# RWKV chunk chain in one product for both heads, and its group norm along the free axis

## The chip, the cores and the metric

The kernel runs on one core of a Trainium2 chip. The metric is the time of one execution on the device in microseconds (us), the median of three runs. The names of the engines are those of the profile: PE is TensorE (PEld its weight loads), DVE is VectorE, ACT is ScalarE, POOL is GpSimd and SP is SyncE, which issues most DMAs.

## The reference

One decoder block with 512 tokens and 2048 channels in fp32: RMS norm, an input projection `w_in`, RWKV-7 time mixing (16 heads of 64) beside sliding-window attention, a gated merge through `w_out`, then a gated ConvFFN. The change touches the RWKV part alone:

```python
def step(state, inp):
    r_t, k_t, v_t, w_t, ka_t, kb_t = inp
    sa = jnp.einsum('bhvk,bhk->bhv', state, ka_t)
    state = (state * w_t[:, :, None, :] + sa[..., None] * kb_t[:, :, None, :]
             + v_t[..., None] * k_t[:, :, None, :])
    y = jnp.einsum('bhvk,bhk->bhv', state, r_t)
    return state, y
...
mu = jnp.mean(y, axis=-1, keepdims=True)
var = jnp.mean(jnp.square(y - mu), axis=-1, keepdims=True)
y = ((y - mu) * lax.rsqrt(var + GN_EPS)).reshape(B, S, RW_DIM)
y = y * gn_w.astype(f32) + gn_b.astype(f32)
bonus = jnp.sum(rh * kh * r_k.astype(f32), axis=-1, keepdims=True) * vh
out = (y + bonus.reshape(B, S, RW_DIM)) * g.astype(f32)
```

The state is 64 x 64 per head; the mean and variance are over a head's 64 channels.

## The kernel before

The 512 columns of a tile are tokens and its 128 partitions channels, that is two heads of 64, a pair; there are `NP` = 8 pairs. The tokens are cut into `NCH` = 8 chunks of `C` = 64. In the stretch of the change TensorE does two kinds of work:

- **The projections.** Each of 70 z tiles (`ztile`, `project`) is 48 products of 128x128 weights with 512 columns into a PSUM tile `acc` (L260, L261, L262: weights and input each in a high and a low part, three products). A weight tile comes by a DMA on SP (`raw`, L240), ACT makes its high part `whi` (L243) and DVE the low part `wlo` (L244); three such pairs of tiles are held, each good for 12 products. After every third weight load `sums_along` issues one copy in DRAM on SP (L227) and one accumulating DMA on POOL that waits for it (L228).
- **The RWKV work of a pair**, in three functions. `early(p)` projects k, r and v, makes the decays and gates, normalises `kk` (its column statistics by `head_stats`, L378, and `head_rows`, L381 and a trip through DRAM). `late(p)` is the chunk algorithm. `final(p)` is the group norm and the output `o_rw_d`.

The loop is `late(p)`, `early(p+1)`, `final(p)`, three gate tiles (`emit_gate`), for each pair. The order on each engine is not the program's: a scheduler fixes it when the kernel is built, from priorities and readiness, so products of the projections are placed between those of the chain; only what `pin` marks keeps its place. Queues run in the order so fixed.

`late(p)` before: it forms `BKK` (keys) and `BAR` (queries, per head `h` and kind `a`, with zeros in the other head's partitions), and for each chunk the product of both (L689, four to a PSUM tile). DVE masks it into `AB` (strictly causal, L692) and `MM` (causal, L693). In each head's half of the partitions the own head's block is copied to `BX` (L698) and its place in `AB` is refilled with `BAR` (L700); so `AB` and `SV` together hold for each head its chunk-crossing and its state part one above the other. `BX` is then inverted by five levels of fp16 products and transposes (L728 to L730, L751). `KK` and the values in `UV` and `SV` come by transposes (L715, L719). The chain is eight serial steps:

- psG (L758): per head a product with 64 output columns of the array, into that head's half of the partitions; DVE copies it to `G` (L760).
- psU (L762): one product with `BX` (block-diagonal); ACT copies one head's half to `UV` (L763), DVE the other (L764).
- psS (L769): per head again; DVE adds it to the decayed state `SV` (L771), one operation per head.

The outputs (L779, L781) are per head too, two products each, channel-major, into one PSUM tile `bulk`; `split` cuts them into `yhl`. `final` centres them by two products with a constant (L789, L790), squares, takes statistics with L378, `rsqrt_small` on DVE, and spreads the factors back over channels with `head_rows`: a transpose (L381), a store and two loads in DRAM on SP; then four DVE operations (L799 to L804). The PSUM ring `bulk` has three tiles, the chain's ring two.

Of the kernel before, what the change touches and what calls it, by code (L numbers as in the profile page):

```python
# [18 lines left out]
P = 128  # L19
# [3 lines left out]
C = 64  # L23
# [11 lines left out]
class Dims:  # L35
# [38 lines left out]
    ("ident", 128), ("strict", 64), ("incl", 64), ("istack", 64),  # L74
    ("m1", 64), ("m2", 64), ("m4", 64), ("m8", 64), ("m16", 64), ("m32", 64),
    ("t1bd", 128), ("idsg", 128), ("tri", 128), ("bo", 128), ("cen", 128), ("sel2", 2), ("ones", 128), ("dist", 256),
# [9 lines left out]
def shape_constants():  # L86
    out = np.zeros((P, NCONST), np.float32)

    def put(nm, a):
        o, n = CONST_AT[nm]  # L90
        out[:, o : o + n] = a

    i = np.arange(P)
    put("ident", np.eye(P))
    s = (i % C)[:, None]
    t = np.arange(C)[None, :]
    put("strict", s < t)
    put("incl", s <= t)
# [10 lines left out]
    put("cen", (si == ti) - same / float(C))  # L109
# [25 lines left out]
def block_kernel(ctx: ExitStack, tc: tile.TileContext, d: Dims, a: dict, out: bass.AP):  # L135
# [136 lines left out]
    bor = cstp.tile([P, P], F32R, name="bor")  # L272
    cenr = cstp.tile([P, P], F32R, name="cenr")
# [9 lines left out]
    if True:  # L283
# [69 lines left out]
        pin(act.activation(bor, K["bo"], AF.Copy))  # L353
        pin(act.activation(cenr, K["cen"], AF.Copy))
# [162 lines left out]
        with ExitStack() as pr:  # L517
# [56 lines left out]
            pool.memset(BAR[0:C, :, 1], 0.0)  # L574
            pool.memset(BAR[C:P, :, 0], 0.0)
            AB, MM, KK, SV, UV = (bd.tile([P, NCH, 2, C], F32, name=n) for n in ("AB", "MM", "KK", "SV", "UV"))
            pool.memset(SV[0:C, 0, 0], 0.0)
            pool.memset(SV[C:P, 0, 1], 0.0)
# [20 lines left out]
            def early(p):  # L599
# [56 lines left out]
                dve.tensor_tensor(bon, vz, ps, op=ALU.mult)  # L656
                return ag, Ei, kk, kb, k2, rz, vz, bon

            def late(p, st):
# [3 lines left out]
                for h, (lo, hi) in enumerate(HV):  # L663
                    ol, oh = HV[1 - h]
                    hs = slice(lo, hi)
                    dve.tensor_tensor(BKK[hs, :, lo:hi], kb3[hs], Ei3[hs], op=ALU.mult)
                    dve.tensor_tensor(BKK[hs, :, ol:oh], k23[hs], Ei3[hs], op=ALU.mult)
                    dve.scalar_tensor_tensor(BAR[hs, :, h, 0], kk3[hs], -1.0, Eex[hs], op0=ALU.mult, op1=ALU.mult)
                    dve.tensor_tensor(BAR[hs, :, h, 1], rz3[hs], Ein[hs], op=ALU.mult)
                    act.activation(BV[hs, :, ol:oh], vz3[hs], AF.Copy)  # L670
# [14 lines left out]
                dve.tensor_tensor(BKE, BKK, ee.unsqueeze(2).to_broadcast([P, NCH, P]), op=ALU.mult)  # L685
                for n0 in range(0, NCH, 2):
                    ps = bulk().rearrange("p (q c) -> p q c", c=P)
                    for j in range(2):
                        pe.matmul(ps[:, 2 * j : 2 * j + 2].rearrange("p q c -> p (q c)"), BKK[:, n0 + j],  # L689
                                  BAR[:, n0 + j].rearrange("p h a c -> p (h a c)"), start=True, stop=True)  # L690
                    q2 = lambda t: t[:, n0 : n0 + 2].rearrange("p n h c -> p (n h) c")
                    dve.tensor_tensor(q2(AB), ps[:, :, 0:C], mb("strict", 4), op=ALU.mult)  # L692
                    dve.tensor_tensor(q2(MM), ps[:, :, C:P], mb("incl", 4), op=ALU.mult)  # L693
                for g in range(2):
                    ns = slice(g * HN, (g + 1) * HN)
                    for h, (lo, hi) in enumerate(HV):
                        own = AB[lo:hi, ns, h]
                        (dve.tensor_copy if h else act.copy)(BX[lo:hi, ns, lo:hi], own)  # L698
                        dve.tensor_tensor(tt[lo:hi, ns], own, mb("m1", HN, (lo, hi)), op=ALU.mult)
                        act.copy(own, BAR[lo:hi, ns, h, 0])  # L700
                    dve.tensor_tensor(tt[:, ns], tt[:, ns], mb("istack", HN), op=ALU.add)
                    split(X[:, 0, ns], X[:, 1, ns], tt[:, ns])
                    ps = bulk().rearrange("p (n c) -> p n c", c=P)
                    for j in range(HN):
                        pe.transpose(ps[:, j], BX[:, g * HN + j], ident)
                    at_ = wk.tile([P, HN, P], F32, name="at_", tag="at_")
                    dve.scalar_tensor_tensor(at_, ps, SG, mb("idsg", HN), op0=ALU.mult, op1=ALU.add)
                    split(AI[:, 0, ns], AI[:, 1, ns], at_)
                    for i in range(2):
                        dve.tensor_tensor(BT[:, i, ns], AI[:, i, ns], mb("t1bd", HN), op=ALU.mult)  # L710
                for g in range(2):
# [43 lines left out]
                for n in range(NCH):  # L755
                    ps = chn.tile([P, C], F32, name="psG", tag="chn")
                    for h, (lo, hi) in enumerate(HV):
                        pe.matmul(ps[lo:hi], AB[:, n, h], SV[:, n, h], start=True, stop=True)  # L758
# [3 lines left out]
                    pe.matmul(ps, BX[:, n], G, start=True, stop=True)  # L762
                    act.activation(UV[0:C, n, 0], ps[0:C], AF.Copy)  # L763
                    dve.tensor_copy(UV[C:P, n, 1], ps[C:P])  # L764
                    if n == NCH - 1:
                        break
                    ps = chn.tile([P, C], F32, name="psS", tag="chn")
                    for h, (lo, hi) in enumerate(HV):
                        pe.matmul(ps[lo:hi], KK[:, n, h], UV[:, n, h], start=True, stop=True)  # L769
                    for h, (lo, hi) in enumerate(HV):  # L770
                        dve.scalar_tensor_tensor(SV[lo:hi, n + 1, h], SV[lo:hi, n, h], ee[lo:hi, n : n + 1], ps[lo:hi],  # L771
                                                 op0=ALU.mult, op1=ALU.add)


                ps = bulk()
                for n in range(NCH):
                    for h, (lo, hi) in enumerate(HV):
                        dst = r3(ps)[lo:hi, n]
                        pe.matmul(dst, UV[:, n, h], MM[:, n, h], start=True, stop=n == 0)  # L779
                        if n:  # L780
                            pe.matmul(dst, SV[:, n, h], BAR[:, n, h, 1], start=False, stop=True)  # L781
                yhl = wk.tile([P, 2, S], F32R, name="yhl", tag="rhl")
                split(yhl[:, 0], yhl[:, 1], ps)
                return ag, bon, yhl

            def final(p, st):
                ag, bon, yhl = st
                ps = bulk()
                pe.matmul(ps, cenr, yhl[:, 0], start=True, stop=False)  # L789
                pe.matmul(ps, cenr, yhl[:, 1], start=False, stop=True)  # L790
                yc = wtile("yc")
                dve.tensor_copy(yc, ps)
                sq = wtile("gn")
                act.activation(sq, ps, AF.Square)
                ps = bulk()
                head_stats(ps, sq)
                rs = rsqrt_small(wk, ps[:, 0 : 2 * NT], 1.0 / HD, GN_EPS)
                rb = head_rows(wk, bulk(), rs, "gn")
                dve.tensor_tensor(yc, yc, rb, op=ALU.mult)  # L799
                dve.tensor_scalar(yc, yc, col("gn_w", p), col("gn_b", p), op0=ALU.mult, op1=ALU.add)  # L800
                dve.tensor_tensor(yc, yc, bon, op=ALU.add)
# [605 lines left out]
```

## Time and profile before

| | |
|---|---|
| median of three runs | 2952.3 us (2951.39 to 2952.68) |
| profiled execution, its span | 2946.4 us |
| TensorE busy | 2897.7 us (98%) |
| VectorE busy | 1949.0 us (66%) |
| ScalarE busy | 1316.0 us (45%) |
| mean granted TensorE clock | 0.997 |
| first psG to last | 352.3 to 1193.5 us |

The profiled execution's time is its span; the median is from other runs. A row of the groups gives line, engine, operation, what it writes and reads, the tile sizes and a count, then busy time and mean ns of one, then idle time before them and what ended it. In the timeline, a row is a start and a length in us; `x4` are four records merged. An fp32 product appears as two records, a product in the projections' format or in fp16, and a transpose, as one. `128*64` is rows and columns of the array that are in use. Records overlap: a start is nearer to the cost than a length.

### The profile page before, as it was taken

To read this page: it belongs to the slowest core of one execution; us is meant where nothing else is said; L and a number is where in the kernel's file an instruction comes from. 1 tells how busy PE (TensorE), PEld (TensorE's weight loads), DVE (VectorE), ACT (ScalarE), POOL (GpSimd) and SP (SyncE) were. 2 spreads that over 40 slices of the span, in tenths; PEclk is the share of its full clock that TensorE was granted. 3 is DMA by queue.
4 is the path that set the end of the run, shared out by engine and by line. 5 is a ranking of instruction groups with operands and counts; after the bars stand their busy time and mean duration, and the time that the engine had idled before them with its cause. 6 is when DMAs were issued, how large, how long until landed. Compare 5 with 4: busy or idle time off the path is not lost.

```text
span 2946.4 us, 48467 instructions
## 1 busy us (share of the span) xinstructions
PE 2897.7 (98%) x18922; PEld 2473.2 (84%) x18922; DVE 1949.0 (66%) x3242; ACT 1316.0 (45%) x2134; POOL 219.4 (7%) x286
## 2 busy tenths in 40 slices
PE   7999999999999999999999899999999999999999
PEld 6777777777777777688888899999999999888887
DVE  5555666666666666344567877778777778665555
ACT  4344434434334334232346554554554555544444
POOL 0001000000000000101000011011011011000000
PEclk9999999999999999999999999999999999999999
DMA  6855656656656656878877788888888888877775
GB/s 185 210 151 153 178 139 154 159 129 161 158 131 162 155 129 170 250 223 262 275 243 247 193 242 236 230 227 225 234 239 235 227 229 237 311 240 242 256 258 189
DMA packets 225142, 609.47 MB, mean 207 GB/s; under 512 B 24768, under 2 KB 44944, under 8 KB 223888
## 3 DMA queue, kind: packets, MB, share of 16 engines
q1 hardware_dynamic: 157504, 434.92, 45.9%
q0 software_dynamic: 36064, 132.14, 23.3%
q10 hardware_dynamic: 31344, 39.31, 3.9%
q8 instruction: 148, 2.42, 0.3%
q14 instruction: 82, 0.67, 0.1%
HBM read 556.62 MB, written 174.43 MB: 248 GB/s over the span
## 4 chain that ended last, share of the span: by engine, by line
PE 92%; DVE 3%; ACT 2%; DMA 2%; issue 1%; ACTq 0%; SPq 0%; DVEq 0%
PE X L1108 17%; PE X L975 11%; PE acc L262 10%; PE acc L261 10%; PE acc L260 10%; PE Y L975 8%; PE Y L1108 8%; PE Z L1108 4%; PE psG L758 1%; PE bulk L689 1%; PE mi L505 1%; PE bulk L751 1%; PE psS L769 1%; PE bulk L728 1%; DMA raw<-in_w_z_dram 1%
## 5 line engine op out<-in xcount | busy, mean ns | idle before, releaser
L262 PE MATMUL acc<-xhi,wlo 128*128 128x512 f32 x1120 | 460.0, 411 | 0.7 <-DVE wlo L244 0.7
L260 PE MATMUL acc<-xhi,whi 128*128 128x512 f32 x1120 | 454.9, 406 | 4.0 <-ACT whi L243 4.0
L261 PE MATMUL acc<-xlo,whi 128*128 128x512 f32 x1120 | 453.9, 405 | 0.0
L243 ACT ACTIVATE whi<-raw 128x512 fp32r<-128x512 f32 x352 | 220.0, 629 | 491.3 <-PE acc L261 326.2
L968 DVE TENSOR_TENSOR wlo<-raw,whi 128x1024 fp32r<-128x1024 f32 x210 | 257.0, 1224 | 203.4 <-ACT whi L967 202.4
L244 DVE TENSOR_TENSOR wlo<-raw,whi 128x512 fp32r<-128x512 f32 x352 | 240.3, 688 | 205.1 <-ACT whi L243 198.1
L967 ACT ACTIVATE whi<-raw 128x1024 fp32r<-128x1024 f32 x210 | 222.6, 1060 | 289.3 <-PE X L975 151.8
L1108 PE MATMUL X<-b,whi 128*128 128x256 f32 x1472 | 270.4, 284 | 2.3 <-DVE u L1128 0.9
L1108 PE MATMUL X<-t,whi 128*128 128x256 f32 x1408 | 258.9, 284 | 8.7 <-DVE u L1128 8.3
L1091 DVE TENSOR_TENSOR wlo<-raw,whi 128x1024 fp32r<-128x1024 f32 x176 | 215.1, 1223 | 77.5 <-ACT whi L1090 77.2
L1108 PE MATMUL Y<-t,whi 128*128 128x256 f32 x1408 | 257.1, 283 | 0.0
L262 PEld LDWEIGHTS acc<-xhi,wlo 128*128 128x128 f32 x1120 | 211.3, 189 | 44.2 <-issue 3.1
L260 PEld LDWEIGHTS acc<-xhi,whi 128*128 128x128 f32 x1120 | 211.6, 189 | 43.2 <-ACT whi L243 5.2
L261 PEld LDWEIGHTS acc<-xlo,whi 128*128 128x128 f32 x1120 | 211.3, 189 | 40.3 <-issue 3.1
L1090 ACT ACTIVATE whi<-a 128x1024 fp32r<-128x1024 f32 x132 | 139.3, 1056 | 216.4 <-DVE a L1084 213.2
L1108 PEld LDWEIGHTS X<-b,whi 128*128 128x128 f32 x1472 | 230.7, 193 | 3.1 <-issue 2.4
L1108 PEld LDWEIGHTS X<-t,whi 128*128 128x128 f32 x1408 | 220.8, 193 | 9.3 <-DVE u L1128 5.7
L1108 PEld LDWEIGHTS Y<-t,whi 128*128 128x128 f32 x1408 | 219.6, 192 | 0.0
L1108 PE MATMUL X<-b,wlo 128*128 128x256 f32 x736 | 209.1, 284 | 2.1 <-DVE wlo L1091 2.1
L1091 DVE TENSOR_TENSOR wlo<-a,whi 128x1024 fp32r<-128x1024 f32 x132 | 161.7, 1226 | 68.2 <-ACT whi L1090 67.6
L1108 PE MATMUL X<-t,wlo 128*128 128x256 f32 x704 | 200.1, 284 | 0.1
L1108 PE MATMUL Y<-t,wlo 128*128 128x256 f32 x704 | 199.2, 283 | 0.0
(346 smaller groups left out, 6151.2 us busy)
## 6 DMA issues: line engine op xcount, KB each, us to landing
raw<-in_w_up_dram SPq DMA_DIRECT2D x180, 512.0 KB
raw<-in_w_z_dram SPq DMA_DIRECT2D x288, 256.0 KB
s_dn<-in_w_dn_dram POOLq DMA_DIRECT2D x88, 512.0 KB, 6.3
raw<-in_w_up_dram POOLq DMA_DIRECT2D x88, 512.0 KB, 8.7
raw<-s_dn SPq DMA_DIRECT2D x88, 512.0 KB
raw<-in_w_dn_dram SPq DMA_DIRECT2D x66, 512.0 KB
a<-in_w_up_dram SPq DMA_DIRECT2D x48, 512.0 KB
s_dn<-in_w_dn_dram SPq DMA_DIRECT2D x44, 512.0 KB
```

The source lines that it names most:

```text
L243: pin(act.activation(hi, raw, AF.Copy))
L244: pin(dve.tensor_tensor(lo, raw, hi.bitcast(F32), op=ALU.subtract))
L260: pe.matmul(acc, whi[:, j], xhi[:, k], start=first, stop=False)
L261: pe.matmul(acc, whi[:, j], xlo[:, k], start=False, stop=False)
L262: pe.matmul(acc, wlo[:, j], xhi[:, k], start=False, stop=last)
L505: pe.matmul(ps[:, h], pT[:, kb, h], vt[:, n - 1 + kb, g * HD : (g + 1) * HD], start=kb == kbs[0], stop=kb == kbs[-1])
L967: act.activation(whi, wr, AF.Copy)
L968: dve.tensor_tensor(wlo, wr, whi.bitcast(F32), op=ALU.subtract)
L975: pe.matmul(dst, l[:, q, ts], r[:, es], start=fst and j == 0, stop=lst and j == 2, skip_group_check=True)
L1090: pin(act.activation(hi, t, AF.Copy))
L1091: pin(dve.tensor_tensor(lo, t, hi.bitcast(F32), op=ALU.subtract))
L1108: pin(pe.matmul(ps, l[:, k], r[:, k], start=start and k + i == 0, stop=last and i == 2, skip_group_check=True))
```

## The change

`AB`, `MM`, `KK`, `SV`, `UV` go. In their place everything of a chunk stands for both heads at once, on 128 partitions, with operands that are block-diagonal or hold a mask's zeros:

- Four masks in place of two split L689's product into `BX` and `OA` (own head's block and the crossing one, strictly causal) and `MD` and `MO` (the same, causal). `BAR` is laid out by kind first, so both heads' queries are one 128-column operand.
- The values are centred over the head's channels at once, and turned to token-major, by a product with a constant (`VV`). What the values add to G (`GV`) and to the state (`KV`) is made in bulk for all eight chunks (`bulk_mm`, copied out by ACT). Since all values are centred, so are the states and outputs.
- In the chain psG, psU and psS are one full-width product each; the first chunk has no psG. `G` is an addition on DVE, psU is copied by ACT in one piece, the decayed state is added to `KV` aside.
- Outputs are token-major: three products a chunk, copied by ACT to `yt`. `final` takes squares and sums along the free axis, scales, and turns the result back to channel-major by eight products with an identity; scale and shift of the group norm are merged with the bonus, to which ACT adds the shift in `early`.
- The tile tag `ko` is shared by `OA`, `KO` and `yd`, the tag `yt` by `GV` and `yt`. `KO` is zeroed by two memsets on POOL for each pair.

```diff
-            AB, MM, KK, SV, UV = (bd.tile([P, NCH, 2, C], F32, name=n) for n in ("AB", "MM", "KK", "SV", "UV"))
+            MO, MD = (bd.tile([P, NCH, P], F32, name=n) for n in ("MO", "MD"))
+            KD = bdtile("KD")
+            SS, UU, VV, KV = (bd.tile([P, NCH, C], F32, name=n) for n in ("SS", "UU", "VV", "KV"))
...
+                act.activation(bon, bon, AF.Identity, bias=col("gn_b", p))
...
-                    dve.tensor_tensor(q2(AB), ps[:, :, 0:C], mb("strict", 4), op=ALU.mult)
-                    dve.tensor_tensor(q2(MM), ps[:, :, C:P], mb("incl", 4), op=ALU.mult)
+                    for t, a, nm in ((BX, 0, "own"), (OA, 0, "other"), (MD, 1, "own"), (MO, 1, "other")):
+                        dve.tensor_tensor(t[:, n0 : n0 + 2], pq[:, :, a], mb(nm, 2)[:, :, a * P : (a + 1) * P], op=ALU.mult)
...
-                        (dve.tensor_copy if h else act.copy)(BX[lo:hi, ns, lo:hi], own)
-                        dve.tensor_tensor(tt[lo:hi, ns], own, mb("m1", HN, (lo, hi)), op=ALU.mult)
-                        act.copy(own, BAR[lo:hi, ns, h, 0])
+                        dve.tensor_tensor(tt[lo:hi, ns], BX[lo:hi, ns, lo:hi], mb("m1", HN, (lo, hi)), op=ALU.mult)
...
+                def bulk_mm(dst, l, r):
+                    ps = bulk()
+                    for n in range(NCH):
+                        pe.matmul(r3(ps)[:, n], l(n), r(n), start=True, stop=True)
+                    act.activation(dst, r3(ps), AF.Copy)
+
+                bulk_mm(VV, lambda n: BV[:, n], lambda n: K["cens"])
+                GV = wk.tile([P, NCH, C], F32, name="GV", tag="yt")
+                bulk_mm(GV, lambda n: OA[:, n], lambda n: VV[:, n])
...
-                    act.activation(KK[:, ns].rearrange("p n h c -> p n (h c)"), ps, AF.Copy)
-                    ps = bulk().rearrange("p (n h c) -> p n h c", h=2, c=C)
-                    for j in range(HN):
-                        pe.transpose(ps[:, j].rearrange("p h c -> p (h c)"), BV[:, g * HN + j], ident)
+                    if g == 0:
+                        KO = wk.tile([P, NCH, P], F32, name="KO", tag="ko")
+                        pool.memset(KO[0:C, :, 0:C], 0.0)
+                        pool.memset(KO[C:P, :, C:P], 0.0)
                     for h, (lo, hi) in enumerate(HV):
-                        act.activation(UV[lo:hi, ns, 1 - h], ps[lo:hi, :, 1 - h], AF.Copy)
-                        act.copy(SV[lo:hi, ns, 1 - h], ps[lo:hi, :, 1 - h])
+                        ol, oh = HV[1 - h]
+                        act.activation(KD[lo:hi, ns, lo:hi], ps[lo:hi, :, lo:hi], AF.Copy)
+                        act.activation(KO[lo:hi, ns, ol:oh], ps[lo:hi, :, ol:oh], AF.Copy)
+
+                bulk_mm(KV, lambda n: KO[:, n], lambda n: VV[:, n])
...
-                    for h, (lo, hi) in enumerate(HV):
-                        pe.matmul(ps[lo:hi], AB[:, n, h], SV[:, n, h], start=True, stop=True)
-                    G = wk.tile([P, C], F32, name="G", tag="G", bufs=2)
-                    dve.tensor_copy(G, ps)
+                    if n:
+                        ps = chn.tile([P, C], F32, name="psG", tag="chn")
+                        pe.matmul(ps, BAR[:, n, 0].rearrange("p h c -> p (h c)"), SS[:, n], start=True, stop=True)
+                        G = wk.tile([P, C], F32, name="G", tag="G", bufs=2)
+                        dve.tensor_tensor(G, GV[:, n], ps, op=ALU.add)
+                    else:
+                        G = GV[:, 0]
...
-                    act.activation(UV[0:C, n, 0], ps[0:C], AF.Copy)
-                    dve.tensor_copy(UV[C:P, n, 1], ps[C:P])
+                    act.activation(UU[:, n], ps, AF.Copy)
...
-                    for h, (lo, hi) in enumerate(HV):
-                        pe.matmul(ps[lo:hi], KK[:, n, h], UV[:, n, h], start=True, stop=True)
-                    for h, (lo, hi) in enumerate(HV):
-                        dve.scalar_tensor_tensor(SV[lo:hi, n + 1, h], SV[lo:hi, n, h], ee[lo:hi, n : n + 1], ps[lo:hi],
-                                                 op0=ALU.mult, op1=ALU.add)
+                    pe.matmul(ps, KD[:, n], UU[:, n], start=True, stop=True)
+                    dve.tensor_tensor(SS[:, n + 1], KV[:, n], ps, op=ALU.add)
...
+                    pe.matmul(dst, MO[:, n], VV[:, n], start=True, stop=False)
+                    pe.matmul(dst, MD[:, n], UU[:, n], start=False, stop=n == 0)
+                    if n:
+                        pe.matmul(dst, BAR[:, n, 1].rearrange("p h c -> p (h c)"), SS[:, n], start=False, stop=True)
+                yt = wk.tile([P, NCH, C], F32, name="yt", tag="yt")
+                act.activation(yt, r3(ps), AF.Copy)
...
+                sq = wk.tile([P, NCH, C], F32, name="gn", tag="gn")
+                act.activation(sq, yt, AF.Square)
+                ss = wk.tile([P, NCH], F32, name="ssy", tag="ssy")
+                dve.reduce_sum(ss, sq, axis=AX.X)
+                rs = rsqrt_small(wk, ss, 1.0 / HD, GN_EPS)
...
+                yd = wk.tile([P, NCH, 2, C], F32, name="yd", tag="ko")
+                for h in range(2):
+                    dve.tensor_tensor(yd[:, :, h], yt, rs2[:, :, h : h + 1].to_broadcast([P, NCH, C]), op=ALU.mult)
                 ps = bulk()
+                for n in range(NCH):
+                    pe.matmul(r3(ps)[:, n], yd[:, n].rearrange("p h c -> p (h c)"), K["istack1"], start=True, stop=True)
+                yc = wtile("gn")
+                dve.scalar_tensor_tensor(yc, ps, col("gn_w", p), bon, op0=ALU.mult, op1=ALU.add)
```

More of the change, by code (lines that the diff above doesn't have):

```diff
@@ L73 @@
 CONST_PARTS = (
-    ("ident", 128), ("strict", 64), ("incl", 64), ("istack", 64),
+    ("ident", 128), ("own", 256), ("other", 256), ("istack", 64), ("istack1", 64),
     ("m1", 64), ("m2", 64), ("m4", 64), ("m8", 64), ("m16", 64), ("m32", 64),
-    ("t1bd", 128), ("idsg", 128), ("tri", 128), ("bo", 128), ("cen", 128), ("sel2", 2), ("ones", 128), ("dist", 256),
+    ("t1bd", 128), ("idsg", 128), ("tri", 128), ("bo", 128), ("cens", 64), ("sel2", 2), ("ones", 128), ("dist", 256),
 )
@@ L96, in shape_constants @@
     t = np.arange(C)[None, :]
-    put("strict", s < t)
-    put("incl", s <= t)
+    both = np.concatenate([s < t, s < t, s <= t, s <= t], axis=1)
+    at_home = np.tile(np.repeat((i // C)[:, None] == np.arange(2)[None, :], C, axis=1), 2)
+    put("own", both & at_home)
+    put("other", both & ~at_home)
+    put("istack1", s == t)
     put("istack", SG * (s == t))
@@ L108, in shape_constants @@
     put("bo", same)
-    put("cen", (si == ti) - same / float(C))
+    put("cens", (s == t) - 1.0 / C)
     put("sel2", si // C == np.arange(2)[None, :])
@@ L352, in block_kernel @@
         xin.close()
-        pin(act.activation(bor, K["bo"], AF.Copy))
-        pin(act.activation(cenr, K["cen"], AF.Copy))
         def ztile(c0):
@@ L573, in block_kernel @@
             BAR = bd.tile([P, NCH, 2, 2, C], F32, name="BAR")
-            pool.memset(BAR[0:C, :, 1], 0.0)
-            pool.memset(BAR[C:P, :, 0], 0.0)
-            AB, MM, KK, SV, UV = (bd.tile([P, NCH, 2, C], F32, name=n) for n in ("AB", "MM", "KK", "SV", "UV"))
-            pool.memset(SV[0:C, 0, 0], 0.0)
-            pool.memset(SV[C:P, 0, 1], 0.0)
+            pool.memset(BAR[0:C, :, :, 1], 0.0)
+            pool.memset(BAR[C:P, :, :, 0], 0.0)
+            MO, MD = (bd.tile([P, NCH, P], F32, name=n) for n in ("MO", "MD"))
+            KD = bdtile("KD")
+            SS, UU, VV, KV = (bd.tile([P, NCH, C], F32, name=n) for n in ("SS", "UU", "VV", "KV"))
             Et = bd.tile([P, NCH, C + 1], F32, name="Et")
@@ L667, in late @@
                     dve.tensor_tensor(BKK[hs, :, ol:oh], k23[hs], Ei3[hs], op=ALU.mult)
-                    dve.scalar_tensor_tensor(BAR[hs, :, h, 0], kk3[hs], -1.0, Eex[hs], op0=ALU.mult, op1=ALU.mult)
-                    dve.tensor_tensor(BAR[hs, :, h, 1], rz3[hs], Ein[hs], op=ALU.mult)
+                    dve.scalar_tensor_tensor(BAR[hs, :, 0, h], kk3[hs], -1.0, Eex[hs], op0=ALU.mult, op1=ALU.mult)
+                    dve.tensor_tensor(BAR[hs, :, 1, h], rz3[hs], Ein[hs], op=ALU.mult)
                     act.activation(BV[hs, :, ol:oh], vz3[hs], AF.Copy)
@@ L685, in late @@
                 dve.tensor_tensor(BKE, BKK, ee.unsqueeze(2).to_broadcast([P, NCH, P]), op=ALU.mult)
+                OA = wk.tile([P, NCH, P], F32, name="OA", tag="ko")
                 for n0 in range(0, NCH, 2):
-                    ps = bulk().rearrange("p (q c) -> p q c", c=P)
+                    ps = bulk()
                     for j in range(2):
[L689 to L692, printed above, removed]
-                    dve.tensor_tensor(q2(MM), ps[:, :, C:P], mb("incl", 4), op=ALU.mult)
+                        pe.matmul(ps[:, j * 4 * C : (j + 1) * 4 * C], BKK[:, n0 + j],
+                                  BAR[:, n0 + j].rearrange("p a h c -> p (a h c)"), start=True, stop=True)
+                    pq = ps.rearrange("p (n a c) -> p n a c", n=2, a=2)
+                    for t, a, nm in ((BX, 0, "own"), (OA, 0, "other"), (MD, 1, "own"), (MO, 1, "other")):
+                        dve.tensor_tensor(t[:, n0 : n0 + 2], pq[:, :, a], mb(nm, 2)[:, :, a * P : (a + 1) * P], op=ALU.mult)
                 for g in range(2):
@@ L710, in late @@
                         dve.tensor_tensor(BT[:, i, ns], AI[:, i, ns], mb("t1bd", HN), op=ALU.mult)
+                def bulk_mm(dst, l, r):
+                    ps = bulk()
+                    for n in range(NCH):
[4 more added lines that the diff above has]
+                bulk_mm(GV, lambda n: OA[:, n], lambda n: VV[:, n])
                 for g in range(2):
@@ L775, in late @@
+                    dve.tensor_tensor(SS[:, n + 1], KV[:, n], ps, op=ALU.add)
                 ps = bulk()
                 for n in range(NCH):
[L777 to L782, printed above, removed]
@@ L783, in late @@
-                split(yhl[:, 0], yhl[:, 1], ps)
-                return ag, bon, yhl
-            def final(p, st):
-                ag, bon, yhl = st
-                ps = bulk()
[L789 to L801, printed above, removed]
+                    dst = r3(ps)[:, n]
```

11 lines of the change are left out of this document (7 added, 4 removed).

## The prediction

> **What bounds the kernel now.** I read the page first, then the waits of TensorE in the stretch that the change touches, then two tables by stretch: one of all engines over five whole pairs of heads, one of a single matmul line over the same stretch.
>
> ```profile
> span 2946.4 us, 48467 instructions
> PE 2897.7 (98%) x18922; PEld 2473.2 (84%) x18922; DVE 1949.0 (66%) x3242; ACT 1316.0 (45%) x2134; POOL 219.4 (7%) x286
> ```
>
> ```profile
> PE bulk L728 <- ACT AI L206: 1.3, 5, 0.3
> PE bulk L381 <- DVE rq L197: 0.8, 5, 0.2
> ```
>
> ```profile
> 451.59:1008.59 557.00, 554.23 (x3901) 416.96 (x3900) 366.46 (x810) 223.13 (x451) 35.62 (x45) 1.00 0.61 150
> 451.59:1008.59 557.00, 199.50 (x481) 90.41 (x480) 1.00 0.61 150
> ```
>
> The stretch runs from one pair's first L689 to that of the fifth pair after it. TensorE is busy 554.23 of 557.00 us at full granted clock and waits only 2.1 us for anything (the two rows are all its waits there); DVE is at 66%, ACT at 40%. So a pair costs 557.0 / 5 = 111.4 us, and its eight pairs get shorter only if TensorE has less to do. The busy figures can't tell how much: records overlap. I go by steps from start to start.
>
> ```profile
> 450.68 0.39 PE L262 MATMUL acc<-xhi,wlo 128*128 128x512 f32 x1
> ...
> 451.59 3.61 PE L689 MATMUL bulk<-BAR,BKK 128*128 128x256 f32 x16
> ...
> 1008.59 3.62 PE L689 MATMUL bulk<-BAR,BKK 128*128 128x256 f32 x16
> ```
>
> Four projection products (acc) begin in 0.91 us: 0.2275 us each, though a record lasts 0.39. A pair holds 288 of them (six z tiles of 48; L262's 481 in the table is 3 x 480 / 3 and one at the edge): 65.5 us. The other 45.9 us are the RWKV work of one pair. What a small product costs is what it pushes the following acc products back:
>
> ```profile
> 504.90 0.40 PE L262 MATMUL acc<-xhi,wlo 128*128 128x512 f32 x1
> 505.22 0.39 PE L769 MATMUL psS<-UV,KK 128*64 128x64 f32 x3
> ...
> 505.83 0.50 PE L260 MATMUL acc<-xhi,whi 128*128 128x512 f32 x1
> 506.17 0.40 PE L261 MATMUL acc<-xlo,whi 128*128 128x512 f32 x1
> 506.50 0.34 PE L758 MATMUL psG<-SV,AB 128*64 128x64 f32 x4
> 506.76 0.50 PE L262 MATMUL acc<-xhi,wlo 128*128 128x512 f32 x1
> 507.10 0.39 PE L260 MATMUL acc<-xhi,whi 128*128 128x512 f32 x1
> 507.33 0.40 PE L261 MATMUL acc<-xlo,whi 128*128 128x512 f32 x1
> 507.56 0.40 PE L262 MATMUL acc<-xhi,wlo 128*128 128x512 f32 x1
> 507.79 0.33 PE L762 MATMUL psU<-G,BX 128*128 128x64 f32 x2
> 507.93 0.48 PE L260 MATMUL acc<-xhi,whi 128*128 128x512 f32 x1
> 508.25 0.27 PE L381 MATMUL bulk<-ident,rq 128*8 128x128 f32 x1
> ```
>
> This is one chunk of the chain. An fp32 product has two records. L762, the one product of the chain that uses the full 128x128 array, is inserted between L262 at 507.56 and L260: two acc products and it take 508.25 - 507.56 = 0.69, so it costs 0.69 - 0.455 = **0.235**. L758, half-width (128*64), both heads side by side: 506.17 to 507.33 holds three acc products, so it costs 1.16 - 0.68 = **0.48**, although its four records start within 0.26. L769 with the outputs L779 and L781 of both heads (12 records): 504.90 to 506.17, 1.27 - 0.455 = **0.81**. An acc product ahead of a half-width one is followed 0.32 or 0.33 us later, not 0.23, and one behind it 0.34 later: entering and leaving the half-width form has a price. It is dearer where the order separates the heads:
>
> ```profile
> 509.19 0.71 PE L621 MATMUL bulk<-wl,thw 128*128 128x128 f32 x4
> 509.83 0.33 PE L758 MATMUL psG<-SV,AB 128*64 128x64 f32 x2
> 510.09 0.49 PE L621 MATMUL bulk<-wl,thw 128*128 128x128 f32 x2
> 510.50 0.33 PE L758 MATMUL psG<-SV,AB 128*64 128x64 f32 x2
> 510.76 0.49 PE L621 MATMUL bulk<-wl,thw 128*128 128x128 f32 x2
> 511.01 0.48 PE L261 MATMUL acc<-xlo,whi 128*128 128x512 f32 x1
> ...
> 1190.08 0.40 PE L262 MATMUL acc<-xhi,wlo 128*128 128x512 f32 x1
> 1190.41 0.33 PE L769 MATMUL psS<-UV,KK 128*64 128x64 f32 x2
> ...
> 1190.90 0.50 PE L260 MATMUL acc<-xhi,whi 128*128 128x512 f32 x1
> 1191.23 0.40 PE L261 MATMUL acc<-xlo,whi 128*128 128x512 f32 x1
> ```
>
> From 509.19 to 511.01 there are eight L621 records at about 0.114 (that step: next fence) and two lone halves of L758: 1.82 - 0.91 = 0.91 for both. One head's L769, L779, L781 alone: 1.15 - 0.455 = 0.69, so 1.39 for both heads.
>
> ```profile
> 1096.02 0.39 PE L262 MATMUL acc<-xhi,wlo 128*128 128x512 f32 x1
> 1096.32 1.05 PE L378 MATMUL bulk<-cst,gn 128*128 128x2 f32 x8
> 1097.23 0.48 PE L260 MATMUL acc<-xhi,whi 128*128 128x512 f32 x1
> 1097.55 0.40 PE L261 MATMUL acc<-xlo,whi 128*128 128x512 f32 x1
> ```
>
> L378 streams two columns a record, yet its eight records with 128x128 weights take 0.91 us: 0.114 each. So in a run, a full-width fp32 record can't go below 0.114, a product not below 0.228, however few columns it streams.
>
> **The change, part by part, per pair of heads, on TensorE.** The half-width products (32 records psG, 28 psS, 32 and 28 of the outputs) go. By the rows above a chunk of them costs between 0.48 + 0.81 = 1.29 and 0.91 + 1.39 = 2.30, eight chunks 10.3 to 18.4. The 45.9 tells where between: the pair's other records (3901 / 5 = 780, less 288 and 120, so 372), added up by their starts in the same way, take about 29.5, which leaves **16.4**. I take that.
>
> In their place stand full-width products: psG 7 and psS 7, lone, at 0.235 = 3.3; outputs 8 MO + 8 MD + 7 BAR = 23 at 0.228 = 5.2. Sum **8.5**.
>
> New: V centred (8), its share of G (8), its share of the state (8), and the turn back to channel-major in the group norm (8): 32 products at 0.228 = 7.3, and for each of some five runs the start that L378's run shows beyond its records (1.53 - 0.455 - 0.91 = 0.165): 0.8. Sum **8.1**.
>
> Gone besides: eight transposes of BV at L378's step, 0.9; the two centring products of 512 columns at the acc step, 0.455; the group norm's L378 run, 1.53 - 0.455 = 1.075; one L381, 0.2 (508.25 to the next record). Sum **2.6**.
>
> Net: 16.4 + 2.6 - 8.5 - 8.1 = 2.4 us a pair, **19 us** over eight. With the ends of the half-width price it is -3.7 to 4.4 a pair: 30 us lost to 35 gained.
>
> A rule of the Trainium skill speaks against the change: "TensorEngine Tiling (Array Packing)", Theoretical Speedup, promises up to twofold speed where a dimension is 64 or less, and the old form used that. The same page's Key Properties state that changing the tiling mode drains the engine; by the rows (0.32 to 0.34 in place of 0.23 at either edge) the trace agrees with this second rule, and in a chain whose products stand singly among full-width ones it decides.
>
> DVE, ACT and the queues, at nothing, since TensorE's acc products cover them:
>
> ```profile
> L692 DVE TENSOR_TENSOR AB<-bulk,cst 128x256 f32<-128x256 f32 x32 | 13.4, 419 | 0.2 <-PE bulk L689 0.2
> L771 DVE SCALAR_TENSOR_TENSOR SV<-SV,ee,psS 64x64 f32<-64x64 f32 x112 | 31.3, 280 | 22.9 <-PE psS L769 18.9 <-PE bulk L779 0.5
> ```
>
> DVE gets 16 mask products of this size for 8 (3.4 us more a pair); the chain loses its UV copy, one of two state updates and the copy of G's first chunk, the group norm swaps four 512-wide operations for about as many, and one split and two BX copies go: about 3 less. ACT loses 14 small copies and two KK copies, and gains three bulk copies, eight KD/KO copies and the bias on the bonus: level. At 66% and 40% neither becomes the bound; uncovered, the mask products would cost at most 8 x 3.4 = 27. The chain gets shorter by a serial DVE copy and a state update per chunk, which gains nothing, as TensorE has acc products to fill it. The group norm's trip through DRAM (one store and two loads a pair on SP) goes; TensorE did not wait for it, so its gain is nothing, and SP's weight loads stand behind three fewer issues. The other queue it touches is POOL's, with two memsets of KO a pair.
>
> The profiled execution spans 2946.4 us, 5.9 below the median 2952.3; I take the difference as unchanged. 2952.3 - 19 = **2933**.
>
> **The rivals.**
>
> *The price of the half-width form is waiting for the chain, and stays.* Then each of the 14 lone products a pair costs what a lone half-width head did, 0.91 / 2 = 0.455, not 0.235: 14 x 0.22 x 8 = 25 back, net +6, 2958; with half to all of the price a wait, 2946 to 2958, about no change. For it: the chain is serial. Against it: L762 is in the same chain and costs 0.235, and the step into the half-width form is 0.32 to 0.33 wherever shown, where a wait would scatter.
>
> *Slower: KO's memset is caught in POOL's queue.* It stands between the share of G and the copy that ACT makes for the share of the state.
>
> ```profile
> POOL s_dn L228 <- DMA s_dn<-in_w_dn_dram: 456.0, 40, 21.1
> ACT whi L243 <- PE acc L261: 115.9, 56, 4.3
> L565 POOL MEMSET BX<- 64x512 f32 x1 | 0.5, 536 | 0.0
> ```
>
> POOL's accumulating DMA waits on average 11.4 us, at worst 21.1, for the copy before it, and a memset behind it waits as long. ACT would stand at KO's copy, and with it the weight splits whi. Up to three weight tiles are ahead, 12 products each: 3 x 12 x 0.2275 = 8.2 us. Beyond that TensorE stands: 3.2 us a pair at the mean wait, 26 over eight, net 2952 + 7 = 2959; at the worst 12.9 a pair, 3036. It decides from 2.4 us a pair. Against it: the memset takes 0.5 and its order on POOL can fall ahead of the wait, and ACT's weight splits mostly wait for TensorE, so they run early.
>
> *Slower: the half-width form is cheap, and any lone product pays at its edges.* The twelve records from 505.22 take until 505.83, way out included: 0.05 each, both heads at once. If nothing else were due to the form, 120 records at 0.05 are 6.0 a pair in place of 16.4: net -8.0 a pair, 64 lost, 3016. The slow steps at the edges are against it. By Theoretical Speedup in the Trainium skill's "TensorEngine Tiling (Array Packing)" it would come out so, 3016 in place of 2933.
>
> *Faster: a full-width record in a run costs 0.07.* L762's two records give way to L260 after 0.14. Then the 23 + 32 products in runs fall from 0.228 to 0.14: 4.8 a pair, 39 us more, 2894. Against it: L378, and the 0.32 that L260 needs behind L762.
>
> **How the numbers follow.** My forecast 0.68, with its own range 2918 to 2945; the wait that stays 0.11; the memset 0.11; cheap half-width 0.04; cheap full-width 0.06. 2933 is the likeliest. Leaving out the two last and the worse part of the memset, the range is 2914 to 2957. A difference of 0.2% (6 us) is about what this kernel's runs can tell from none. Faster holds my forecast, the cheap full-width case and 0.01 of the rest; same, most of the wait that stays; slower, the memset, the cheap half-width and the end of the wait: 0.75, 0.10, 0.15.
>
> **What would show it.** Five pairs should take some 545 us, TensorE still over 99% busy there; psG and psS appear as two records of 128*128 with the next acc step but one back at 0.23; the new runs step by 0.114. POOL's memsets should end within 2 us of the share of G. The forecast is wrong if TensorE's waits in the pairs pass 2 us each, if whi comes late behind KO, or if acc products beside psG still step by 0.32.

## The result and the profile after

The changed kernel takes 2937.65 us (median; before 2952.49): the ratio of the runs is 0.9943, 95% interval 0.993 to 0.9956, and the medians differ by 15 us. The forecast was 2933, 19 less. The profiled execution spans 2935.8 us.

The page of the changed kernel, then TensorE's waits and the row of all engines over the same five pairs as before (from one pair's first product of `BAR` and `BKK`, now L690, to that of the fifth after it; columns: stretch, length, busy us and records of PE, PEld, DVE, ACT and POOL, granted clock, DMA share, GB/s):

```profile
span 2935.8 us, 48494 instructions
PE 2885.4 (98%) x18914; PEld 2520.2 (86%) x18914; DVE 1934.4 (66%) x3202; ACT 1312.2 (45%) x2100; POOL 228.0 (8%) x302
```

```profile
PE bulk L809 <- DVE yd L806: 3.7, 5, 0.8
```

```profile
452.77:998.60 545.83, 541.63 (x3897) 443.10 (x3895) 356.46 (x785) 221.27 (x431) 40.64 (x55) 1.00 0.62 150
```

Five pairs take 545.83 us in place of 557.00: 109.17 a pair for 111.4, **2.2 us less where 2.4 was forecast**. TensorE has as many records as before (3897 for 3901) and is as full; it still waits for almost nothing (3.7 us, for the scaled outputs `yd` in the group norm). The busy columns show nothing of the gain's cause: PE's falls by about as much as the time (12.6 us for 11.2), and PEld's even rises. The chain in the timeline (start, length, records):

```profile
514.75 0.40 PE L265 MATMUL acc<-xhi,wlo 128*128 128x512 f32 x1
514.99 0.40 PE L263 MATMUL acc<-xhi,whi 128*128 128x512 f32 x1
515.22 0.33 PE L780 MATMUL psS<-UU,KD 128*128 128x64 f32 x2
515.39 0.39 PE L787 MATMUL bulk<-UU,MD 128*128 128x64 f32 x2
515.62 0.39 PE L789 MATMUL bulk<-SS,BAR 128*128 128x64 f32 x2
515.84 0.39 PE L786 MATMUL bulk<-VV,MO 128*128 128x64 f32 x2
516.03 0.48 PE L264 MATMUL acc<-xlo,whi 128*128 128x512 f32 x1
516.35 0.39 PE L265 MATMUL acc<-xhi,wlo 128*128 128x512 f32 x1
516.58 0.39 PE L263 MATMUL acc<-xhi,whi 128*128 128x512 f32 x1
516.81 0.33 PE L767 MATMUL psG<-SS,BAR 128*128 128x64 f32 x2
516.95 0.48 PE L264 MATMUL acc<-xlo,whi 128*128 128x512 f32 x1
517.27 0.40 PE L265 MATMUL acc<-xhi,wlo 128*128 128x512 f32 x1
```

The step from an acc product into psG is 0.23 where it was 0.32 to 0.33. The step of the acc product behind psG is still 0.32 (516.95 to 517.27): that one stands behind any small product, full-width L762 of the kernel before included, so it was no sign of the half-width form. psG between L263 at 516.58 and L265 at 517.27 costs 0.69 - 0.455 = 0.235, as forecast; psS with three outputs, 514.99 to 516.35, costs 1.36 - 0.455 = 0.905 for eight records, 0.113 each.

The run of the centred V, and the start of the first pair, where the gain is lost again:

```profile
460.17 0.39 PE L264 MATMUL acc<-xlo,whi 128*128 128x512 f32 x1
460.40 1.89 PE L712 MATMUL bulk<-cst,BV 128*128 128x64 f32 x16
462.10 0.48 PE L265 MATMUL acc<-xhi,wlo 128*128 128x512 f32 x1
462.42 0.39 PE L263 MATMUL acc<-xhi,whi 128*128 128x512 f32 x1
...
340.64 1.97 PE L690 MATMUL bulk<-BAR,BKK 128*128 128x256 f32 x8 [0.39 <-DVE BAR L669]
...
345.20 1.13 PE L690 MATMUL bulk<-BAR,BKK 128*128 128x256 f32 x4 [2.14 <-DVE bon L655]
```

Sixteen records of a run cost 462.42 - 460.17 - 0.455 = 1.795: 0.112 each. The first pair begins 1.8 us later than before (340.64 for 338.87) and takes 112.1 us (452.77 less 340.64) where it took 112.7, so it gains 0.6 and not 2.2. Part of that varies: in a second profile of the changed kernel (`after_again`) the pair begins at 339.64 and takes 113.8, with the granted clock at half for 3.4 us in it.

### The profile page after: what moved, and what is told of

Same layout as the page of the kernel before. It is cut to its first block, busy times and chain, and to the rows that moved or that the text cites. A ratio compares the mean times of both kernels' runs of the same rounds, so it can differ in the third digit from the quotient of the medians.

```text
span 2935.8 us, 48494 instructions
## 1 busy us (share of the span) xinstructions
PE 2885.4 (98%) x18914; PEld 2520.2 (86%) x18914; DVE 1934.4 (66%) x3202; ACT 1312.2 (45%) x2100; POOL 228.0 (8%) x302
## 4 chain that ended last, share of the span: by engine, by line
PE 90%; DVE 4%; DMA 2%; issue 1%; ACT 1%; ACTq 0%; SPq 0%; DVEq 0%; POOLq 0%
PE X L1118 16%; PE X L985 11%; PE acc L265 10%; PE acc L263 10%; PE acc L264 10%; PE Y L985 8%; PE Y L1118 8%; PE Z L1118 4%; PE bulk L712 1%; PE bulk L690 1%; PE bulk L760 1%; DMA raw<-in_w_up_dram 1%; PE mi L504 1%; PE bulk L737 1%; PE acc L326 1%
## 5 line engine op out<-in xcount | busy, mean ns | idle before, releaser
L263 PE MATMUL acc<-xhi,whi 128*128 128x512 f32 x1120 | 454.8, 406 | 2.0 <-ACT whi L246 2.0
L265 PE MATMUL acc<-xhi,wlo 128*128 128x512 f32 x1120 | 453.2, 405 | 0.2
L263 PEld LDWEIGHTS acc<-xhi,whi 128*128 128x128 f32 x1120 | 211.6, 189 | 40.7 <-ACT whi L246 2.9
L265 PEld LDWEIGHTS acc<-xhi,wlo 128*128 128x128 f32 x1120 | 211.6, 189 | 39.8 <-issue 3.1
```

The costliest lines, as they stand in the source:

```text
L263: pe.matmul(acc, whi[:, j], xhi[:, k], start=first, stop=False)
L265: pe.matmul(acc, wlo[:, j], xhi[:, k], start=False, stop=last)
```

## The experiments

All but `after_again` are edits of the changed kernel; times are set against its medians, 2937.4 to 2937.7, and a pair's length, from the row of five pairs, against its 109.17.

**Chain in half-width form.** `half_chain`:

```diff
-    pe.matmul(ps, BAR[:, n, 0].rearrange("p h c -> p (h c)"), SS[:, n], start=True, stop=True)
+    for h, (lo, hi) in enumerate(HV):
+        pe.matmul(ps[lo:hi], BAR[:, n, 0, h], SS[:, n], start=True, stop=True)
...
-    pe.matmul(ps, KD[:, n], UU[:, n], start=True, stop=True)
+    for h, (lo, hi) in enumerate(HV):
+        pe.matmul(ps[lo:hi], KD[:, n, lo:hi], UU[:, n], start=True, stop=True)
```

> The changed kernel, but psG and psS made as two products of 64 output columns, one per head (128*64 in place of 128*128), same operands, same waits. Theory (going into and out of the half-width form costs TensorE time): each of the 14 products a pair costs 0.48 (heads side by side) to 0.91 (apart) in place of 0.235, so 3.4 to 9.4 us a pair, 27 to 76 us over eight: 2965 to 3013 us, and acc products beside psG follow 0.32 to 0.34 after, not 0.23. Rival (the price before was waiting for the chain): the waits are the same, so no more than 5 us: 2933 to 2943. Rival (half-width records are cheap, lone products pay at any edge): 28 half records of 0.05 for 28 full ones of 0.114, so 1 to 2 us a pair less: 2922 to 2930.

Measured: 2958.37 us, 21 more; ratio to the kernel before 1.0016 (1.0007 to 1.0026). The five pairs:

```profile
455.75:1016.15 560.40, 556.09 (x4036) 440.15 (x4035) 357.47 (x785) 221.66 (x431) 40.70 (x55) 1.00 0.59 146
```

```profile
520.89 0.40 PE L263 MATMUL acc<-xhi,whi 128*128 128x512 f32 x1
521.22 0.34 PE L768 MATMUL psG<-SS,BAR 128*64 128x64 f32 x4
521.49 0.50 PE L264 MATMUL acc<-xlo,whi 128*128 128x512 f32 x1
521.82 0.39 PE L265 MATMUL acc<-xhi,wlo 128*128 128x512 f32 x1
```

Operands and waits are those of the changed kernel; only the form differs. The step of 0.33 into psG is back, from psG to the next acc product it is 0.27 where it was 0.14, and the step behind that hardly moves (0.33 for 0.32): 521.82 - 520.89 - 0.455 = 0.475, for 0.235. A pair costs 112.08, 2.9 more, 0.21 for each of the 14 products. That is under the range (3.4 to 9.4 a pair), near its lower end: with both heads' operands from one operation, the halves always stand together. The theory of waits expected no more than 5 us and the one of cheap half-width products a gain; both fall.

**Outputs in half-width form.** `half_out`, the chain as in the change:

```diff
-    dst = r3(ps)[:, n]
-    pe.matmul(dst, MO[:, n], VV[:, n], start=True, stop=False)
+    for h, (lo, hi) in enumerate(HV):
+        dst = r3(ps)[lo:hi, n]
+        pe.matmul(dst, MO[:, n, lo:hi], VV[:, n], start=True, stop=False)
...
```

> The changed kernel, but the outputs made as two products of 64 output columns, one per head; the chain stays full-width. Theory (the price is at the edges of the form, so few of them are cheap): 92 half records of about 0.05 replace 46 of 0.114, level, and each visit to the form costs about 0.3: eight to sixteen visits a pair, 2.4 to 4.8 us, 19 to 38 us over eight: 2957 to 2976 us. If records of the form were dear in themselves, 92 at 0.13 against 46 at 0.114 would be 6.7 a pair, 54 us: 2990 or more. Rival (half-width is cheap, heads run side by side): no loss, 2930 to 2940.

Measured: 2937.98 us, no change. So the form was not dear there, against my expectation: the rival's number came out. A pair has twice the output records and takes 109.56 us, 0.4 more. Call a stretch of half-width records without a full-width one between them a visit to the form. In the timelines the chain's 56 half records a pair lie in 14 visits, the outputs' 92 in 9. With what they replace (14 lone products at 0.235; 46 records at 0.114) and the measured differences (2.9 and 0.4), two unknowns fit both runs: 56 r + 14 v = 6.2 and 92 r + 9 v = 5.6 give **0.03 us a half record and 0.33 us a visit**. By this fit half-width is cheap while both heads run side by side and dear each time it is entered and left. Two unknowns always fit two runs; `half_bulk` and `half_out_last` test it.

**Bulk products twice.** `double_bulk` makes each of the 32 twice (`for _ in range(2):` ahead of the product in `bulk_mm` and in `final`).

> The changed kernel with each of the 32 bulk products a pair (centred V, its share of G and of the state, the turn back in the group norm) made twice. Theory (a full-width fp32 record in a run costs one weight load, 0.114): 64 more records, 7.3 us a pair, 58 us over eight: 2993 to 2999 us. Rival (0.07 a record): 36 us, 2974. Rival (TensorE has slack in the pairs, the chain sets their length): under 15 us, below 2953.

Measured: 3001.54 us, 64 more, ratio 1.0155 (1.014 to 1.017). That is 2.5 us above the expected range. TensorE has no slack in the pairs. Two of the five pairs had the granted clock at half for 6.8 us each, for which the theory had no term; here is one of them, and the pair after it:

```profile
577.94:697.87 119.93, 118.82 (x845) 98.00 (x844) 71.73 (x157) 44.23 (x87) 8.32 (x12) 0.97 0.55 136
697.87:814.49 116.62, 115.50 (x844) 95.75 (x843) 71.75 (x157) 44.22 (x87) 8.14 (x11) 1.00 0.57 141
```

At full clock a pair takes 116.6, 7.5 more than the changed kernel's: 0.117 for each of the 64 added records, as the theory had it and far from 0.07.

**KO's zeroing off GpSimd's queue.** `ko_dve` has `dve.memset` for the two `pool.memset`.

> The changed kernel with the two zeroings of KO a pair on VectorE in place of GpSimd's queue. Theory (TensorE does not wait for KO, GpSimd's queue costs nothing): within 4 us of the changed kernel, 2934 to 2942. Rival (the zeroing is caught behind the waiting accumulating DMA and holds ScalarE): some us faster, below 2933.

Measured: 2940.86 us, 3 more, within what was expected. In the changed kernel POOL's memset does stand in the queue, but waits for the share of G itself:

```profile
POOL s_dn L231 <- DMA s_dn<-in_w_dn_dram: 438.2, 39, 22.2
...
POOL KO L725 <- PE bulk L712: 15.1, 3, 5.7
...
POOL KO L725 <- DVE BT L708: 12.2, 2, 7.5
```

In every pair both zeroings have ended 1.2 to 1.3 us after the last product of the share of G (465.01 to 466.30 in the second), so no waiting DMA holds them, and TensorE waits for no KO. The rival of the memset falls.

**The changed kernel once more.** `after_again`, unedited:

> The changed kernel once more, as the base of the next run. 2935 to 2940 us; its profile tells whether the stages after the pairs, which the change leaves alone, vary by some us from one execution to the next.

Measured: 2937.41 us. A pair takes 109.16 us, as in the first profile. The untouched remainder from the merge's last `ahi` product to the end took 1525.0 us here, 1523.3 in the first profile of the changed kernel and 1519.5 in that of before. The granted clock was at half for 12 us of that stretch in the profile of before and for 17 to 18 in the two others, which is some 3 us of the difference. So profiled spans of the same code vary by some 5 us there, and the spans' difference of 10.6 understates the change.

**V turned by transposes.** `v_turned`: eight transposes and two DVE operations for eight fp32 products, and seven products in the share of the state:

```diff
-                bulk_mm(VV, lambda n: BV[:, n], lambda n: K["cens"])
+                for g in range(2):
...
+                        pe.transpose(ps[:, j], BV[:, g * HN + j], ident)
...
+                dve.reduce_sum(vm, VV, axis=AX.X)
+                dve.scalar_tensor_tensor(VV, vm.unsqueeze(2).to_broadcast([P, NCH, C]), -1.0 / C, VV, op0=ALU.mult, op1=ALU.add)
```

> The changed kernel with V turned to token-major by eight transposes (one record each) and centred by two VectorE operations in place of eight fp32 products (two records each), and without the eighth product of the share of the state, which nothing reads. Theory (TensorE's records set the pairs' length at about 0.11 each): 8 + 2 records less, 1.1 us a pair, 9 us over eight: 2926 to 2931 us, a ratio of about 0.997 to the changed kernel. Rival (VectorE's two added operations of 0.69 us or the chain set the pace): no gain or a loss, 2936 or more.

Measured: 2958.57 us, 21 slower; the rival was right in sign, and in part of the cause. The waits over five pairs and their row:

```profile
PE bulk L712 <- DVE VV L725: 8.1, 5, 1.6
PE psG L777 <- DVE SS L791: 5.2, 5, 1.2
PE bulk L819 <- DVE yd L816: 3.0, 5, 0.6
...
451.15:1011.95 560.80, 543.84 (x3847) 441.39 (x3846) 360.81 (x795) 225.06 (x446) 41.50 (x55) 0.99 0.60 146
```

Ten records a pair are gone (3847 for 3897 over five) and the pair takes 112.16, 3.0 more. DVE's load is hardly higher (360.81 for 356.46); what costs is the place of the two centring operations in its fixed order:

```profile
464.17 0.68 DVE L724 TENSOR_REDUCE vm<-VV 128x8 f32<-128x512 f32 x1
464.76 0.69 DVE L210 TENSOR_TENSOR AI<-at__4590,AI 128x512 f16<-128x512 f32 x1
465.36 1.29 DVE L708 TENSOR_TENSOR BT<-AI,cst 128x512 f16<-128x512 f16 x2
466.57 0.69 DVE L725 SCALAR_TENSOR_TENSOR VV<-vm,VV 128x512 f32<-128x512 f32 x1
```

V's last transposes on TensorE give way at 460.51, and over twenty acc products follow them; but DVE does the second centring (L725) behind other work only at 466.57, and GV, the next on TensorE, starts at 467.40 after a wait of 1.6. One psG a pair waits for its state as well. The three waits are 3.3 us a pair, where the changed kernel has 0.7. A saved record is worth nothing where the fixed order leaves a wait uncovered.

The granted clock adds to it. In three of the five pairs it stood at half for 3.4 us, each time from 18.0 us into the pair, 1.8 behind the end of the wait for VV; acc products there step by 0.42. The last pair without and the first with it:

```profile
562.71:673.75 111.04, 107.94 (x771) 87.40 (x769) 72.14 (x159) 44.95 (x90) 8.25 (x11) 1.00 0.60 148
673.75:786.38 112.63, 109.26 (x771) 88.86 (x770) 72.13 (x159) 45.06 (x90) 8.33 (x11) 0.98 0.61 146
```

Of the 4.1 between the 1.1 expected and the 3.0 lost, the added waits are 2.6 and the clock 1.0 a pair; about 0.5 stays open, and so does why the clock fell, since two pairs with the same waits kept it.

**Half-width form in runs.** `half_bulk` splits the 32 bulk products into one of 64 output columns per head:

```diff
-                        pe.matmul(r3(ps)[:, n], l(n), r(n), start=True, stop=True)
+                        for lo, hi in HV:
+                            pe.matmul(r3(ps)[lo:hi, n], l(n)[:, lo:hi], r(n), start=True, stop=True)
...
```

> The changed kernel with its 32 bulk products a pair each made as two of 64 output columns, one per head, side by side; chain and outputs stay full-width. Theory (fitted to the runs with half-width chain and half-width outputs: 0.03 us a half record while both heads run side by side, 0.33 for each visit to the form): 128 records and some five visits, 5.5 us a pair for 8.1, so 21 us less than the changed kernel: 2911 to 2922 us. Rival (a half record costs 0.058 also beside the other head's): 9.1 us a pair, 8 us more: 2942 to 2948.

Measured: 2925.91 us, 12 less, above the expected range; ratio 0.9917 (0.9899 to 0.9936). A pair takes 108.15 us, 1.0 less where 2.6 were forecast: 8 of the 21 us. The other 4 of the medians' difference are not in the pairs. The run of V, as shown of the changed kernel:

```profile
460.77 0.39 PE L264 MATMUL acc<-xlo,whi 128*128 128x512 f32 x1
461.08 1.15 PE L713 MATMUL bulk<-cst,BV 128*64 128x64 f32 x32
462.17 0.50 PE L265 MATMUL acc<-xhi,wlo 128*128 128x512 f32 x1
462.50 0.40 PE L263 MATMUL acc<-xhi,whi 128*128 128x512 f32 x1
...
468.25 0.69 PE L713 MATMUL bulk<-VV,KO 128*64 128x64 f32 x16
...
469.54 0.69 PE L713 MATMUL bulk<-VV,KO 128*64 128x64 f32 x16 [0.26 <-ACT KO L731]
```

32 half records cost 462.50 - 460.77 - 0.455 = 1.275 with their visit, where 16 full ones cost 1.795; 32 x 0.03 + 0.33 = 1.29. The prices hold for this run. What falls short is the rest: the share of the state comes in two visits of 16 records, the second behind a wait, and the turn back in the group norm still waits for `yd` and is split into 2 records and 30, so there are six visits and not five.

**Outputs in one run.** `half_out_last`: half-width outputs, last chunk first and pinned in that order, so that they come in one run behind the chain:

```diff
-                for n in range(NCH):
-                    dst = r3(ps)[:, n]
...
+                for n in reversed(range(NCH)):
+                    terms = [(lambda h, lo, hi: MD[:, n, lo:hi], UU[:, n]), (lambda h, lo, hi: MO[:, n, lo:hi], VV[:, n])]
...
+                            pin(pe.matmul(r3(ps)[lo:hi, n], w(h, lo, hi), x, start=k == 0, stop=k == len(terms) - 1))
```

> The changed kernel with the outputs as half-width products and kept in one run after the chain (92 records, one visit a pair). Theory: 92 x 0.03 + 0.33 = 3.1 us a pair for 5.2, 17 us less: 2917 to 2925. Rival (0.058 a record): level, 2938 to 2942. Rival (the chain sets the pair's length, so later outputs delay it): 2945 or more.

Measured: 2922.21 us, 15 less, ratio 0.99 (0.9885 to 0.9914), inside the range. A pair takes 107.85 us, 1.3 less where 2.1 were forecast, so 10 or 11 of the 15 us are in the pairs. The outputs' records themselves take 2.2 us less by their starts, as the theory had it; of what is lost again two things show: 55 acc products a pair stand right behind a small product where 48 did, and TensorE has a new wait for `lw`, 2.2 us over five pairs. A part of the run, two products of both heads to a row:

```profile
519.15 0.40 PE L263 MATMUL acc<-xhi,whi 128*128 128x512 f32 x1
519.48 0.34 PE L790 MATMUL bulk<-UU,MD 128*64 128x64 f32 x4
519.65 0.29 PE L790 MATMUL bulk<-VV,MO 128*64 128x64 f32 x4
519.76 0.29 PE L790 MATMUL bulk<-SS,BAR 128*64 128x64 f32 x4
...
522.10 0.29 PE L790 MATMUL bulk<-VV,MO 128*64 128x64 f32 x4
522.31 1.05 PE L377 MATMUL bulk<-cst,lg 128*128 128x2 f32 x8
```

From 519.65 to 522.10 there are 21 steps of four records, 0.117 a step, 0.029 a record; the way in shows again as 0.33. A full-width product of both heads takes two records, 0.228; the same as two halves side by side 0.117.

**Both.** `half_bulk_out`:

> Both of these: half-width bulk products, and half-width outputs in one run. If the two gains are TensorE time they add: 34 to 42 us less than the changed kernel, 2896 to 2904. If something else sets the pace by then (DVE, the chain), less than their sum.

Measured: 2912.5 us, 25 less, ratio 0.9863 (0.9846 to 0.9879). That is 8 us above the expected range. A pair takes 106.59 us, 2.6 less, where the two alone gave 1.0 and 1.3: the gains add, so TensorE still sets the pace, and the forecast was too high because those of the two runs were.

**And without the unread product.** `best`:

> As the last one, without the eighth product of the share of the state, which nothing reads: four half records less a pair, about 1 us over eight: 2895 to 2904, not to be told from the last one.

Measured: 2911.1 us, ratio 0.9861 (0.9846 to 0.9876): not to be told from the last one, above the expected range like it, and about 26 us faster than the change. Its five pairs:

```profile
448.70:980.80 532.10, 526.38 (x4426) 410.02 (x4425) 356.88 (x785) 221.81 (x431) 40.66 (x55) 1.00 0.60 154
```

106.4 us a pair with 885 records, where the kernel before took 111.4 with 780.

## Why the prediction was right, point by point

- **TensorE's work sets the pairs' length**: right. Waits stay under 1 us a pair, and doubled products cost their full price (`double_bulk`).
- **Full-width price, 0.235 lone and 0.114 a record in a run**: right; the trace after shows 0.235, 0.113 and 0.112.
- **Half-width price, 16.4 us a pair**: as a sum right, since 2.2 us a pair came of 2.4. It was what the pair's measured length left over, so it holds whatever it is made of. That the form as such costs time in lone products is shown by `half_chain`. But I priced the form as one thing. Put back into the changed kernel, chain and outputs in half-width cost 2.9 and 0.4 a pair, 3.3 of the 7.9 (16.4 less 8.5) that I had set to the form. The kernel before had 28 visits a pair by the same count; 28 x 0.33 and 120 x 0.03 are 12.8 of its 16.4. That its two heads became ready at different times, so that one ran alone and more visits were made, fits the separated rows of before but was not tried alone; 3.6 us a pair stay open. I also took the step of 0.34 behind a half-width product for its way out; 0.32 of it stand behind a full-width one too.
- **The outputs in full-width form, 5.2 us a pair, as part of the gain**: a mistake of choice, not of size. In one run they are cheaper in half-width (`half_out_last`).
- **The rule against the change** was put aside too quickly. The Trainium skill's "TensorEngine Tiling (Array Packing)", Theoretical Speedup, promises up to twofold speed where a dimension is 64 or less. Inside a visit the trace agrees: 0.117 against 0.228 for a product of both heads. Key Properties on that page of the Trainium skill state that changing the tiling mode drains the engine. At the edges the trace agrees: about 0.33 a visit. By the runs, which wins depends on how many records stand together.
- **DVE, ACT and the queues at nothing**: right. DVE's load falls by 2 us a pair (356.46 for 366.46 over five) where I had it level, and TensorE's one wait for it, `yd`, is 0.7 a pair. The first pair is another matter: it begins 1.8 us later and waits 2.1 us inside L690 for DVE's `bon`, where it waited 1.3. The mask products are not the reason: one stands ahead of `bon` on DVE, as before, but DVE is 2.6 us later already at L666 (336.69 for 334.05), ahead of all of them. Why is not shown.
- **Sum**: 8 x 2.23 = 17.9 us, less 3.4 in the first pair, is 14.5; the medians differ by 15. What was off is "over eight": the first pair gains 0.6 less 1.8, not 2.4. The late start is not shown to be the change's work: the second profile of the same kernel begins the pair 0.8 late, not 1.8.
- **Rivals**: waits that stay, the memset, cheap half-width for lone products, and full-width records at 0.07 are excluded by `half_chain`, by `ko_dve` with the trace of the zeroings, by `half_chain` and by `double_bulk` in turn.

## What to carry to other kernels

Where TensorE is full, price a small product by what it pushes back (start to start of the steady products around it), not by its busy time. Lone products among full-width ones belong in full width; products that come in bulk are cheaper split over both halves of the array, kept together in one run. And before a product is saved by work on another engine, look at what the fixed order leaves to cover the new wait.

## What of the hardware was not expected

Two half-width fp32 products of 64 columns, one for each half of the array, take 0.117 us together in a run (`half_out_last`) where one full-width product takes 0.228, although both have 128 rows of weights and 64 columns to stream; entering and leaving the form costs about 0.33, of which 0.09 is the late step that a full-width small product leaves behind it too (0.32 for 0.23). A longer list of records (885 a pair for 780) was the faster kernel. And the granted clock of a core that works alone, with TensorE at least 97% busy, fell to half for some us in single pairs (`double_bulk`, `v_turned`): a difference of a few us between two profiles can be the clock's, and pairs at full clock are the ones to compare.
